# A two-layer encoder on one core: passes over zeros at the start, zero-filled keys, products in runs, new orders

## The chip, the cores and the metric

The kernel runs on one core of a Trainium2 chip. The metric is the device time of one execution in microseconds (us). Three runs of the kernel before took 853.88, 853.45 and 851.22 us; their median is 853.45 us. One more execution was taken with the hardware profiler and has its own time, 852.3 us, of which 850.5 us lie between its first and its last instruction (the span).

## The reference, cut to what matters

256 tokens of 1024 channels go through two layers and a last norm, all in float32.

```python
for i in range(2):
    h = rms_norm(x, norm_mix[i])
    x = x + (even_mixer(h, ...) if i == 0 else odd_mixer(h, ...))
    x = x + cross_attention(rms_norm(x, norm_cross[i]), mem_n, wq, wkv, wo)   # 4 heads, 256 memory tokens
    x = x + square(relu(rms_norm(x, norm_mlp[i]) @ w_up)) @ w_down            # 1024 -> 4096 -> 1024
return rms_norm(x, final_norm)

def even_mixer(h, ...):              # one projection, two groups of its columns
    hy, cq, ckv, kr = split(h @ w_in)
    z = hyena(short_conv(hy))        # two gated long convolutions, done here as products with a DFT table
    o = latent_attention(rms_norm(cq) @ w_uq, rms_norm(ckv) @ w_ukv, kr)      # 8 heads
    return concat(z, o) @ w_out

def odd_mixer(h, ...):               # 8 heads, each with two maps over 64 channels
    q, k, v = split(h @ w_qkv); q, k = rope(q), rope(k)
    p = softmax(q @ k^T / 8)         # 16 maps of 256 x 256
    a = p[:, 0] - lam * p[:, 1]      # the two maps of a head
    return (rms_norm(a @ v) * 0.8...) @ w_out
```

## The kernel before, in words

Every float32 matrix is split into a high and a low part of type fp32r (`split`: ScalarE, called ACT in the profile, rounds to the high part; VectorE, called DVE, subtracts it to get the low part). A product is three passes over TensorE (PE): high by high, high by low, low by high (`mm3`, lines 113 to 117). Each pass loads a block of 128 columns as weights (PEld in the profile) and streams up to 512 columns past it into a PSUM bank. Weights come from HBM by DMA on SyncE's queue (SP), are split, and are held in small rings of buffers (`weight`, line 91).

Where the activations are the weights' partner, their high and low parts lie side by side, so that one pass of 512 columns with the high weights (line 229) and one of 256 columns with the low weights (line 225) do the work of three (`side_by_side`). `proj_w4` makes four output banks so, in four quarters of the contraction: per bank and 128 rows of the contraction a 512-column pass H is followed by a 256-column pass L, and at the last 128 rows L stands before H. It serves the up-projections of both MLPs (8 each) and the queries of both cross-attentions (2 each); `mem_k2` does the same for the keys of the first cross-attention.

The first stage is `lat_proj` (line 496). x arrives in four pieces, the weights of the latent projection in four quarters (`lat_raw`, line 154), all on SyncE's queue. For each quarter `tr_gain` transposes two blocks of 128 channels of x on PE into one PSUM bank and takes them out with the norm's gain on ACT and DVE; the quarter of the weights is split; the products of the quarter before follow. ACT squares and sums the rows of x (line 509), GpSimd (POOL) turns the sums into 1/rms (lines 510, 511, tile `rs0`), and PE spreads `rs0` over a block (line 514) before the first chunk of the hyena projection (`hy_chunk`, H0) starts. `latents` squares the latents with `rs0` as scale (line 528).

What follows is written as lists of letters (`ORDER_EVEN`, `ORDER_CROSS`, `ORDER_ODD`); each letter calls one step. The lists set the order in which the steps are recorded; a scheduler then interleaves them, and what stands on each engine is executed in that order, each instruction waiting for its inputs.

In the odd mixer, `qkv` brings queries and keys to a form with channels on partitions: 128 partitions hold the two maps of a head, 64 each. `od_a` (A) makes the scores of one head: for each half of the tokens and each map an `mm3` over 64 rows and 256 columns, 12 passes, into one bank for each map; then the two softmaxes and the difference. B multiplies by the values, C norms, W is the output projection.

Of the kernel before, what the change touches and what calls it, by code (L numbers as in the profile page):

```python
# [17 lines left out]
P = 128  # L18
D = 1024
# [15 lines left out]
ORDER_ODD = "Q2 Q0 Q1 A0 A1 B0 A2 C0 B1 B2 Q4 C1 C2 Q3 A3 A4 Q5 A5 B3 B4 C3 A6 C4 B5 B6 C5 A7 W0 W1 C6 B7 C7"  # L35
# [3 lines left out]
def tile_encoder(ctx: ExitStack, tc: tile.TileContext, a: dict, out: bass.AP):  # L39
# [102 lines left out]

    pack = const(cst, "cpack", [P, 184])
# [22 lines left out]
    zero = T(cst, [P, 1], F32, "zero")  # L166
    nc.gpsimd.memset(zero, 0.0)
    junk = T(cst, [P, D], BF16, "junk")
# [38 lines left out]
    def proj_x(h, half, k0, nk, n, banks, first, last):  # L207
        hh, hl = h[:2]
        wh, wl = (v3(z[:, :nk * n], nk) for z in half)
        for k in range(nk):  # L210
            for t in range(2):
                sl = (slice(None), k0 + k, slice(t * P, (t + 1) * P))
                mm3(banks[t][:, :n], (hh[sl], hl[sl]), (wh[:, k, :], wl[:, k, :]),
                    first and k == 0, last and k == nk - 1)
# [8 lines left out]
    def side_by_side(b, w, both, kk):  # L223
        def low():
            nc.tensor.matmul(b[:, :256], w[1], both[:, kk, 0, :], start=False, stop=False)  # L225

        if kk == 7:
            low()
        nc.tensor.matmul(v3(b, 2), w[0], both[:, kk], start=kk == 0, stop=kk == 7)  # L229
        if kk < 7:  # L230
            low()

    def proj_w4(h, src, banks, gi, mid=None):
        both = h[2]
        for i in range(4):
            wh, wl = (v3(z, 2) for z in weight(src[i], gi=(gi, 2 * i)))
            for c in range(4):
                for k in range(2):
                    side_by_side(banks[c], [z[:, k, c * P:(c + 1) * P] for z in (wh, wl)], both, 2 * i + k)
            if mid is not None and i == 0:  # L240
                mid()
# [52 lines left out]
    def mem_k2(l, u):  # L294
        bs = [wk(), wk()]
        for i in range(2):
            wh, wl = (v3(z, 4) for z in weight(a["xa_wk"][l, u, i]))
            for c in range(2):
                for k in range(4):
                    side_by_side(bs[c], [z[:, k, c * P:(c + 1) * P] for z in (wh, wl)], memB, 4 * i + k)  # L300
# [129 lines left out]
    def softmax_e(sc, scale=None):  # L430
# [6 lines left out]
        su = col(2)  # L437
# [46 lines left out]

    def tr_gain(u):
        b = hb()
        for k in range(2 * u, 2 * u + 2):
            for t in range(2):
                o = (k % 2) * 256 + t * P
                nc.tensor.transpose(b[:, o:o + P], xt[t][:, k * P:(k + 1) * P], ident)  # L490
        for k in range(2 * u, 2 * u + 2):
            z, g = b[:, (k % 2) * 256:(k % 2 + 1) * 256], gcol[:, 0, k:k + 1]
            nc.scalar.activation(h[0][:, k, :], z, AF.Identity, bias=zero, scale=g)
# [62 lines left out]
    hs = {}  # L556
# [298 lines left out]
    qkT = {}  # L855

    def qkv(i):
# [23 lines left out]
        for u in range(2):  # L881
# [5 lines left out]
            dT = [T(op, [P, 2, 256], F32R, f"qkT{part}{i_}", bufs=3) for i_ in range(2)]  # L887
            split(*dT, b)
# [4 lines left out]
    def od_a(hd):  # L893
# [5 lines left out]
        es_, su = [], []  # L899
        bs = [wk(), wk()]  # L900
# [5 lines left out]
        for b in bs:  # L906
            e3, s_ = softmax_e(b)
            es_.append(e3)
            su.append(s_)
        w = col(2)  # L910
        nc.vector.reciprocal(w, su[1])
        nc.vector.scalar_tensor_tensor(w, w, nlam, su[0], op0=ALU.mult, op1=ALU.mult)
        eps = T(op, [P, 2], F32, "eps", bufs=4)
        nc.vector.scalar_tensor_tensor(eps, su[0], SUBLN_EPS, su[0], op0=ALU.mult, op1=ALU.mult)
        for t in range(2):
            nc.vector.scalar_tensor_tensor(a3[:, t, :], es_[1][:, t, :], w[:, t:t + 1], es_[0][:, t, :],
# [183 lines left out]
```

## Time and profile before

| | |
|---|---|
| median of three runs | 853.45 us |
| profiled execution | 852.3 us |
| its span | 850.5 us |
| PE busy | 829.4 us, 98% |
| DVE busy | 586.6 us, 69% |
| ACT busy | 508.2 us, 60% |
| POOL busy | 19.5 us, 2% |

The busy time of PE counts a pass from its start to its modelled end, and passes overlap: a 512-column pass is shown with 0.39 us while the next starts 0.23 us after it. What a pass costs in a stream is therefore the distance between two starts. The PE has its first pass at 4.60 us and works to 844.9 us; the last 5 us are the final norm and the output's DMA.

### The profile page before, as it was taken

To read this page: it belongs to the slowest core of one execution; us is meant where nothing else is said; L and a number is where in the kernel's file an instruction comes from. 1 tells how busy PE (TensorE), PEld (TensorE's weight loads), DVE (VectorE), ACT (ScalarE), POOL (GpSimd) and SP (SyncE) were. 2 spreads that over 40 slices of the span, in tenths; PEclk is the share of its full clock that TensorE was granted. 3 is DMA by queue.
4 is the path that set the end of the run, shared out by engine and by line. 5 is a ranking of instruction groups with operands and counts; after the bars stand their busy time and mean duration, and the time that the engine had idled before them with its cause. 6 is when DMAs were issued, how large, how long until landed. Compare 5 with 4: busy or idle time off the path is not lost.

```text
span 850.5 us, 12079 instructions
## 1 busy us (share of the span) xinstructions
PE 829.4 (98%) x4514; PEld 695.0 (82%) x4514; DVE 586.6 (69%) x940; ACT 508.2 (60%) x883; POOL 19.5 (2%) x51
## 2 busy tenths in 40 slices
PE   6999999999999999999999999999999999999996
PEld 5867587788888888888888788889998888888885
DVE  4978796876658666666668888677654776666663
ACT  5896464766447555555567667666543755555542
POOL 0010000000000000000000010100000000000000
PEclk9999999999999999999999999999999999999998
DMA  7660317765527666666647416245522566656641
GB/s 275 199 207 19 121 36 263 236 209 159 170 68 218 202 187 190 192 191 186 196 132 226 153 66 198 75 145 178 159 90 100 168 201 189 189 191 184 191 125 50
DMA packets 39519, 138.89 MB, mean 163 GB/s; under 512 B 4515, under 2 KB 5155, under 8 KB 39461
## 3 DMA queue, kind: packets, MB, share of 16 engines
q1 hardware_dynamic: 39460, 138.13, 51.6%
q8 instruction: 35, 0.57, 0.3%
q14 instruction: 24, 0.19, 0.1%
HBM read 137.06 MB, written 1.05 MB: 162 GB/s over the span
## 4 chain that ended last, share of the span: by engine, by line
PE 79%; issue 11%; ACT 4%; DVE 2%; DMA 2%; POOL 1%; SPq 0%; POOLq 0%; ACTq 0%; DVEq 0%
PE h L115 12%; PE h L116 12%; PE h L117 12%; PE b L229 11%; PE b L225 5%; PE h L229 4%; PE f L229 3%; PE b L115 2%; PE h L225 2%; PE b L116 2%; PE b L117 2%; PE f L115 2%; PE f L116 2%; PE f L117 2%; PE f L225 2%
## 5 line engine op out<-in xcount | busy, mean ns | idle before, releaser
L111 DVE TENSOR_TENSOR wlo<-wraw,whi 128x1024 fp32r<-128x1024 f32 (+1 forms) x127 | 153.9, 1218 | 100.9 <-ACT whi L110 100.3
L110 ACT CAST whi<-wraw 128x1024 fp32r<-128x1024 f32 (+1 forms) x127 | 132.5, 1048 | 124.0 <-PE f L229 42.7
L105 ACT ACTIVATE whi<-wraw,zero,cpack 128x512 fp32r<-128x512 f32 x208 | 160.0, 811 | 62.6 <-PE h L117 20.3
L106 DVE SCALAR_TENSOR_TENSOR wlo<-wraw,cpack,whi 128x512 fp32r<-128x512 f32 x208 | 150.3, 749 | 42.8 <-ACT whi L105 42.6
L229 PE MATMUL b<-t,whi 128*128 128x512 f32 x336 | 119.5, 398 | 0.0
L117 PE MATMUL h<-whi,ul 128*128 128x512 f32 x256 | 99.9, 390 | 0.0
L115 PE MATMUL h<-whi,uh 128*128 128x512 f32 x256 | 99.6, 389 | 0.0
L116 PE MATMUL h<-wlo,uh 128*128 128x512 f32 x256 | 99.6, 389 | 0.0
L225 PE MATMUL b<-t,wlo 128*128 128x256 f32 x336 | 87.3, 280 | 0.0
L115 PE MATMUL h<-whi,t 128*128 128x512 f32 x192 | 76.8, 401 | 0.0
L116 PE MATMUL h<-wlo,t 128*128 128x512 f32 x192 | 76.5, 399 | 0.0
L117 PE MATMUL h<-whi,t 128*128 128x512 f32 x192 | 76.0, 397 | 0.0
L229 PEld LDWEIGHTS b<-t,whi 128*128 128x128 f32 x336 | 61.1, 188 | 12.2
L229 PE MATMUL h<-t,whi 128*128 128x512 f32 x192 | 67.9, 400 | 1.4 <-DVE t L111 1.4
L225 PEld LDWEIGHTS b<-t,wlo 128*128 128x128 f32 x336 | 63.4, 189 | 3.7
L116 PEld LDWEIGHTS h<-wlo,uh 128*128 128x128 f32 x256 | 48.0, 188 | 10.1
L117 PEld LDWEIGHTS h<-whi,ul 128*128 128x128 f32 x256 | 48.1, 188 | 9.9
L115 PEld LDWEIGHTS h<-whi,uh 128*128 128x128 f32 x256 | 48.1, 188 | 9.3
L225 PE MATMUL h<-t,wlo 128*128 128x256 f32 x192 | 50.0, 281 | 0.0
L229 PE MATMUL f<-t,whi 128*128 128x512 f32 x112 | 42.7, 398 | 0.0
L117 PEld LDWEIGHTS h<-whi,t 128*128 128x128 f32 x192 | 36.1, 188 | 7.2 <-DVE t L111 0.2
L115 PEld LDWEIGHTS h<-whi,t 128*128 128x128 f32 x192 | 36.1, 188 | 7.0
(325 smaller groups left out, 1633.1 us busy)
## 6 DMA issues: line engine op xcount, KB each, us to landing
wraw<-in_mlp_up_dram SPq DMA_DIRECT2D x64, 512.0 KB, 4.2
wraw<-in_mlp_down_dram SPq DMA_DIRECT2D x64, 512.0 KB, 4.3
wraw<-in_od_w_qkv_dram SPq DMA_DIRECT2D x24, 512.0 KB, 4.3
wraw<-in_xa_wq_dram SPq DMA_DIRECT2D x16, 512.0 KB, 4.1
wraw<-in_xa_wo_dram SPq DMA_DIRECT2D x16, 512.0 KB, 4.2
wraw<-in_w_hy_dram SPq DMA_DIRECT2D x12, 512.0 KB, 4.0
wraw<-in_w_out_ev_dram SPq DMA_DIRECT2D x8, 512.0 KB, 4.4
wraw<-in_xa_wv_dram SPq DMA_DIRECT2D x8, 512.0 KB, 5.4
```

Source lines behind the costliest of these rows:

```text
L105: nc.scalar.activation(h_, r_, AF.Identity, bias=zero, scale=g)
L106: nc.vector.scalar_tensor_tensor(l_, r_, g, h_.bitcast(F32), op0=ALU.mult, op1=ALU.subtract)
L110: nc.scalar.copy(hi, src)
L111: nc.vector.tensor_tensor(lo, src, hi.bitcast(F32), op=ALU.subtract)
L115: nc.tensor.matmul(o, lh, rh, start=first, stop=False)
L116: nc.tensor.matmul(o, lh, rl, start=False, stop=False)
L117: return nc.tensor.matmul(o, ll, rh, start=False, stop=last)
L225: nc.tensor.matmul(b[:, :256], w[1], both[:, kk, 0, :], start=False, stop=False)
L229: nc.tensor.matmul(v3(b, 2), w[0], both[:, kk], start=kk == 0, stop=kk == 7)
```

## The change

Five things. (1) A tile of zeros (`junk`) is set by POOL first, and PE makes 8 passes of 512 columns over it before x is there, and 6 more after the first quarter of x. ACT runs one tiny activation at the start, so that its table is loaded then, and the four quarters of the latent weights are asked for on ACT's queue. Each block of x gets its own bank in `tr_gain`. The first hyena features are made after the third quarter's products, and the squares of x are held back until after the last gain on ACT (`tc.issue_after`). (2) `side_by_side` now makes runs: within a quarter all H passes of the four banks and then all L passes, in the next quarter L before H; in the last quarter it goes bank by bank. (3) The keys of the odd mixer are stored with zeros (`apart`): map 0 fills partitions 0 to 63 of the first 256 columns, map 1 partitions 64 to 127 of the second 256, and the rest is zero. One `mm3` of 128 rows and 512 columns then gives both maps of a head for one half of the tokens: 6 passes per head in place of 12, and the bank holds both maps of 128 tokens in place of one map of 256. (4) Writing the keys so takes two splits of 64 partitions where there was one of 128, and POOL sets six tiles of 128x1024 to zero. (5) The lists of letters change at a few places.

```diff
-ORDER_EVEN = "X J H0 L U K G R S0 D H1 F0 S1 T0 S2 S3 P0 O0 O1 O2 H2 S4 O3 H3 T1 F1 S5 S6 O4 O5 Y S7 H4 P1 H5 O6 O7 M W"
+ORDER_EVEN = "X J H0 L U K R S0 G D H1 F0 S1 T0 S2 P0 S3 O0 O1 O2 H2 S4 O3 H3 T1 F1 S6 S5 O4 O5 Y S7 H4 P1 H5 O6 O7 M W"
-    "Q0 V0 K0 K1 S0 B0 K2 S1 Q1 K3 S2 W0 V2 B1 S3 B2 B3 W1",
+    "Q0 V0 K0 K2 S0 K1 B0 V2 S1 Q1 K3 S2 B1 W0 S3 B2 B3 W1",
-ORDER_ODD = "... Q3 A3 A4 Q5 A5 B3 B4 C3 A6 C4 B5 B6 C5 A7 W0 W1 C6 B7 C7"
+ORDER_ODD = "... Q3 A3 A4 Q5 B3 A5 B4 C3 A6 C4 B6 B5 C5 A7 W0 W1 C6 B7 C7"
...
+    nc.gpsimd.memset(junk[:, :640], 0.0)
+    nc.scalar.activation(T(cst, [P, 1], F32, "first"), zero, AF.Identity, bias=zero, scale=1.0)
+    def wake(n):
+        b = hb()
+        for i in range(n):
+            nc.tensor.matmul(b, junk[:, :128], junk[:, 128:640], start=i == 0, stop=i == n - 1)
+    wake(8)
...
-            nc.sync.dma_start(lat_raw[i], a["w_lat"][i])
+            nc.scalar.dma_start(lat_raw[i], a["w_lat"][i])
...
-    def side_by_side(b, w, both, kk):
...
+        every = range(len(banks))
+        for cs in [(c,) for c in every] if last else [every]:
+            for one in (low, high) if k0 // nk % 2 else (high, low):
+                for c in cs:
+                    for k in range(nk):
+                        one(c, k)
...
+            if q == 0:
+                wake(6)
             if q:
-                proj_x(h, ws[q - 1], 2 * (q - 1), 2, 416, lat, q == 1, False)
-            if q == 2:
-                features_1()
+                z = proj_x(h, ws[q - 1], 2 * (q - 1), 2, 416, lat, q == 1, False)
+        with tc.issue_after(z.ins):
+            features_1()
         proj_x(h, ws[3], 6, 2, 416, lat, False, True)
         ssq = col(2)
-        for t in range(2):
-            nc.scalar.activation(junk, xt[t], AF.Square, accum_out=ssq[:, t:t + 1])
+        with tc.issue_after(hs["X"].ins):
+            for t in range(2):
+                nc.scalar.activation(junk, xt[t], AF.Square, accum_out=ssq[:, t:t + 1])
...
+                dT = apart[(2 * j + u) % 3]
+                for m in range(2):
+                    half = slice(64 * m, 64 * m + 64)
+                    split(*(z[half, :, m * 256:(m + 1) * 256] for z in dT), b[half])
...
-        for t in range(2):
-            for m in range(2):
-                rows = slice(64 * m, 64 * m + 64)
-                mm3(bs[m][:, t * 256:(t + 1) * 256], [z[rows, c, t * P:(t + 1) * P] for z in q], [z[rows, c, :] for z in k],
-                    True, True)
+        for t in range(2):
+            b = wk()
+            mm3(b, [z[:, c, t * P:(t + 1) * P] for z in q], [z[:, c, :] for z in k], True, True)
+            es_.append(softmax_e(b, None, su[:, t, :])[0])
```

ACT in the first stage, before: the squares (L509) stand between the gains (L493) and the splits of the latent weights, and the casts of the first hyena weights (`wraw`, 128x1024) among the last gains.

```order
L509 ACTIVATE junk_90,col_44_228<-t_2_72 128x1024
L493 ACTIVATE t_5_75<-h_129,zero_88,cpack_70 128x256
L110 CAST whi_163<-t_6_76 128x832
L493 ACTIVATE t_5_75<-h_154,zero_88,cpack_70 128x256
L110 CAST whi_200<-t_6_76 128x832
L509 ACTIVATE junk_90,col_44_228<-t_3_73 128x1024
L493 ACTIVATE t_5_75<-h_154,zero_88,cpack_70 128x256
L493 ACTIVATE t_5_75<-h_191,zero_88,cpack_70 128x256
L110 CAST whi_241<-wraw_239 128x1024
L493 ACTIVATE t_5_75<-h_191,zero_88,cpack_70 128x256
L110 CAST whi_271<-wraw_269 128x1024
```

The same place now (L506 are the gains, L525 the squares, `wraw_262` and `wraw_292` the two halves of the first hyena weights):

```order
L110 CAST whi_211<-t_10_91 128x832
L110 CAST whi_264<-wraw_262 128x1024
L110 CAST whi_294<-wraw_292 128x1024
L506 ACTIVATE t_9_90<-h_201,zero_70,cpack_85 128x256
L506 ACTIVATE t_9_90<-h_206,zero_70,cpack_85 128x256
L525 ACTIVATE junk_72,col_51_251<-t_6_87 128x1024
L110 CAST whi_382<-wraw_380 128x768
L525 ACTIVATE junk_72,col_51_251<-t_7_88 128x1024
L110 CAST whi_388<-wraw_386 128x768
L544 ACTIVATE t_63_334,col_61_332<-b_126,rs_19_110 128x256
```

Both casts of the hyena weights now stand ahead of the last two gains, and both squares behind them. On PE the pass that spreads `rs0` still stands between the last latent product and H0.

PE in an up-projection of the first MLP, before (`b` and `f` are output banks, `t` the activations):

```order
L229 MATMUL b_2827<-t_491_2395,whi_2833 128x512
L225 MATMUL b_2827<-t_491_2395,wlo_2834 128x256
L229 MATMUL b_2828<-t_491_2395,whi_2833 128x512
L225 MATMUL b_2828<-t_491_2395,wlo_2834 128x256
L229 MATMUL b_2828<-t_491_2395,whi_2833 128x512
L225 MATMUL b_2828<-t_491_2395,wlo_2834 128x256
```

and now (L239 is H, L243 is L; two rows in one are the two blocks of the quarter):

```order
L239 MATMUL b_2850<-t_498_2418,whi_2856 128x512 x2
L239 MATMUL b_2851<-t_498_2418,whi_2856 128x512 x2
L239 MATMUL b_2852<-t_498_2418,whi_2856 128x512 x2
L239 MATMUL f_2853<-t_498_2418,whi_2856 128x512 x2
L243 MATMUL b_2850<-t_498_2418,wlo_2857 128x256 x2
L243 MATMUL b_2851<-t_498_2418,wlo_2857 128x256 x2
L243 MATMUL b_2852<-t_498_2418,wlo_2857 128x256 x2
L243 MATMUL f_2853<-t_498_2418,wlo_2857 128x256 x2
```

Eight H in a row, then eight L. Over the whole program the places where an L directly follows an H fall from 611 to 107 of 704.

PE at the scores of one head in the odd mixer, before (half of a head's 12 passes, between passes of the projection):

```order
L117 MATMUL h_4890<-whi_4953,t_774_3977 128x512
L115 MATMUL b_4974<-qkT_935_4678,qkT_961_4808 128x256
L116 MATMUL b_4974<-qkT_936_4679,qkT_961_4808 128x256
L117 MATMUL b_4974<-qkT_935_4678,qkT_962_4809 128x256
L115 MATMUL b_4974<-qkT_935_4678,qkT_961_4808 128x256
L116 MATMUL b_4974<-qkT_936_4679,qkT_961_4808 128x256
L117 MATMUL b_4974<-qkT_935_4678,qkT_962_4809 128x256
L115 MATMUL h_5166<-whi_5172,t_800_4100 128x512
```

and now (half of a head's 6 passes):

```order
L905 MATMUL b_4826<-cpack_85,t_958_4805 128x128
L115 MATMUL b_4837<-apart_813_4130,qT_854_4339 128x512
L116 MATMUL b_4837<-apart_814_4131,qT_854_4339 128x512
L117 MATMUL b_4837<-apart_813_4130,qT_855_4340 128x512
L116 MATMUL h_4889<-wlo_4934,t_781_4000 128x512
```

Three passes of 512 columns over all 128 rows stand where six of 256 columns over 64 rows stood.

## Rows read from the trace of the kernel before

**Rows 1.** The page, part 1: busy us, share and instructions.
```profile
PE 829.4 (98%) x4514; PEld 695.0 (82%) x4514; DVE 586.6 (69%) x940; ACT 508.2 (60%) x883; POOL 19.5 (2%) x51
```

**Rows 2.** PE's timeline, first 24 us: start us, us, what.
```profile
4.60 2.04 PE L490 MATMUL h<-cpack,t 128*128 128x128 f32 x8 [4.60 <-DMA t<-in_x_dram]
...
13.63 0.55 PE L117 MATMUL b<-whi,t 128*128 128x416 f32 x1
...
15.79 0.35 PE L117 MATMUL b<-whi,t 128*128 128x416 f32 x1
...
23.18 0.36 PE L115 MATMUL h<-t,whi 128*128 128x256 f32 x1
```

**Rows 3.** Timeline of all engines, 6 to 24 us: ACT, POOL, SP.
```profile
7.37 0.56 ACT L493 ACTIVATE t<-h,zero,cpack 128x256 fp32r<-128x256 f32 x1
...
8.90 0.97 SPq L95 DMA_DIRECT2D wraw<-in_w_hy_dram  x2
...
15.88 1.05 ACT L509 ACTIVATE junk<-t 128x1024 bf16<-128x1024 f32 x1
...
17.40 0.71 POOL L511 TENSOR_TENSOR rs<-col,mhalf 128x2 f32<-128x2 f32 x1
...
18.95 1.04 ACT L110 CAST whi<-wraw 128x1024 fp32r<-128x1024 f32 x1
```

**Rows 4.** DMA issues at 9.5 us: the second hyena half.
```profile
wraw<-in_w_hy_dram SPq DMA_DIRECT2D x1, 512.0 KB, 7.0
```

**Rows 5.** PE's waits in the whole span: total us, times, longest.
```profile
PE b L115 <- ACT t L553: 0.9, 1, 0.9
PE b L117 <- DVE latT L111: 0.8, 1, 0.8
...
PE b L115 <- ACT t L110: 0.7, 1, 0.7
```

**Rows 6.** PE's timeline, one up-projection, 289.17 to 300.43 us.
```profile
289.17 0.39 PE L229 MATMUL b<-t,whi 128*128 128x512 f32 x1
...
297.64 0.40 PE L229 MATMUL b<-t,whi 128*128 128x512 f32 x1
...
298.58 0.39 PE L225 MATMUL b<-t,wlo 128*128 128x256 f32 x2
298.80 0.63 PE L229 MATMUL b<-t,whi 128*128 128x512 f32 x2
299.27 0.40 PE L225 MATMUL b<-t,wlo 128*128 128x256 f32 x2
...
300.43 0.39 PE L115 MATMUL h<-whi,uh 128*128 128x512 f32 x1
```

**Rows 7.** The page, part 5: weight loads of the L passes.
```profile
L225 PEld LDWEIGHTS b<-t,wlo 128*128 128x128 f32 x336 | 63.4, 189 | 3.7
```

**Rows 8.** PE's timeline at two blocks of scores, odd mixer.
```profile
476.23 0.40 PE L116 MATMUL h<-wlo,t 128*128 128x512 f32 x1
...
476.78 0.28 PE L117 MATMUL b<-qkT,qkT 64*128 64x256 f32 x1
476.79 0.28 PE L116 MATMUL b<-qkT,qkT 64*128 64x256 f32 x1
...
478.06 0.50 PE L117 MATMUL h<-whi,t 128*128 128x512 f32 x1
...
479.55 0.39 PE L117 MATMUL h<-whi,t 128*128 128x512 f32 x1
479.87 0.38 PE L115 MATMUL b<-qkT,qkT 64*128 64x256 f32 x1
...
480.78 0.50 PE L115 MATMUL h<-whi,t 128*128 128x512 f32 x1
481.12 0.39 PE L116 MATMUL h<-wlo,t 128*128 128x512 f32 x1
```

**Rows 9.** Odd mixer: PE, PEld, DVE, ACT, POOL busy, clock, DMA.
```profile
455.00:560.00 105.00, 104.34 (x575) 84.40 (x574) 83.44 (x163) 68.05 (x164) 7.55 (x16) 1.00 0.43 134
```

More of the change, by code (lines that the diff above doesn't have):

```diff
@@ L141, in const @@
         return t
+    zero = T(cst, [P, 1], F32, "zero")
+    nc.gpsimd.memset(zero, 0.0)
+    junk = T(cst, [P, D], BF16, "junk")
+    nc.gpsimd.memset(junk[:, :640], 0.0)
[5 more added lines that the diff above has]
+    wake(8)
     pack = const(cst, "cpack", [P, 184])
@@ L212, in proj_x @@
                 sl = (slice(None), k0 + k, slice(t * P, (t + 1) * P))
-                mm3(banks[t][:, :n], (hh[sl], hl[sl]), (wh[:, k, :], wl[:, k, :]),
-                    first and k == 0, last and k == nk - 1)
+                z = mm3(banks[t][:, :n], (hh[sl], hl[sl]), (wh[:, k, :], wl[:, k, :]),
+                        first and k == 0, last and k == nk - 1)
+        return z
     def proj_xs(h, src, n, banks, gi=None, mid=None, at=0):
@@ L221, in proj_xs, with side_by_side, high, low @@
                 mid()
-    def side_by_side(b, w, both, kk):
[L224 to L231, printed above, removed]
+    def side_by_side(banks, w, both, k0):
+        wh, wl = w
+        nk = wh.shape[1]
+        last = k0 + nk == 8
+        def high(c, k):
+            nc.tensor.matmul(v3(banks[c], 2), wh[:, k, c * P:(c + 1) * P], both[:, k0 + k],
+                             start=k0 + k == 0, stop=last and k == nk - 1)
+        def low(c, k):
+            nc.tensor.matmul(banks[c][:, :256], wl[:, k, c * P:(c + 1) * P], both[:, k0 + k, 0, :],
+                             start=False, stop=False)
+        every = range(len(banks))
[4 more added lines that the diff above has]
+                        one(c, k)
     def proj_w4(h, src, banks, gi, mid=None):
-        both = h[2]
         for i in range(4):
[L236 to L239, printed above, removed]
+            w = [v3(z, 2) for z in weight(src[i], gi=(gi, 2 * i))]
+            side_by_side(banks, w, h[2], 2 * i)
             if mid is not None and i == 0:
@@ L296, in mem_k2 @@
         for i in range(2):
[L297 to L300, printed above, removed]
+            side_by_side(bs, [v3(z, 4) for z in weight(a["xa_wk"][l, u, i])], memB, 4 * i)
         y = joined(*bs)
@@ L436, in softmax_e @@
         e3 = v3(t2(), 2)
-        su = col(2)
+        su = col(2) if su is None else su
         for m in range(2):
@@ L483, in tile_encoder @@
     rs0 = T(ep, [P, 2], F32, "rs0")
+    hs = {}
     def tr_gain(u):
-        b = hb()
         for k in range(2 * u, 2 * u + 2):
+            z, g = hb()[:, :256], gcol[:, 0, k:k + 1]
             for t in range(2):
[L489 to L493, printed above, removed]
+                nc.tensor.transpose(z[:, t * P:(t + 1) * P], xt[t][:, k * P:(k + 1) * P], ident)
+            hs["X"] = nc.scalar.activation(h[0][:, k, :], z, AF.Identity, bias=zero, scale=g)
             nc.vector.scalar_tensor_tensor(h[1][:, k, :], z, g, h[0][:, k, :].bitcast(F32), op0=ALU.mult, op1=ALU.subtract)
@@ L855, in tile_encoder @@
     qkT = {}
+    apart = [[T(op, [P, 2, 512], F32R, f"apart{i}{j}", bufs=1) for j in range(2)] for i in range(3)]
+    for z in apart:
+        for y in z:
+            nc.gpsimd.memset(y.bitcast(F32), 0.0)
     def qkv(i):
@@ L886, in qkv @@
                     nc.tensor.transpose(b[:, c, t * P:(t + 1) * P], rows[t][:, cs], ident)
-            dT = [T(op, [P, 2, 256], F32R, f"qkT{part}{i_}", bufs=3) for i_ in range(2)]
-            split(*dT, b)
+            if part == 0:
+                dT = [T(op, [P, 2, 256], F32R, f"qT{i_}", bufs=3) for i_ in range(2)]
+                split(*dT, b)
+            else:
+                dT = apart[(2 * j + u) % 3]
+                for m in range(2):
+                    half = slice(64 * m, 64 * m + 64)
+                    split(*(z[half, :, m * 256:(m + 1) * 256] for z in dT), b[half])
             qkT[part, 2 * j + u] = dT
@@ L898, in od_a @@
         a3 = v3(av, 2)
[L899 to L900 removed]
+        es_ = []
+        su = T(op, [P, 2, 2], F32, "su", bufs=4)
         for t in range(2):
[L902 to L909 removed]
+            b = wk()
+            mm3(b, [z[:, c, t * P:(t + 1) * P] for z in q], [z[:, c, :] for z in k], True, True)
+            es_.append(softmax_e(b, None, su[:, t, :])[0])
         w = col(2)
[L911 to L912 removed]
+        nc.vector.reciprocal(w, su[:, :, 1])
+        nc.vector.scalar_tensor_tensor(w, w, nlam, su[:, :, 0], op0=ALU.mult, op1=ALU.mult)
         eps = T(op, [P, 2], F32, "eps", bufs=4)
[L914 removed]
+        nc.vector.scalar_tensor_tensor(eps, su[:, :, 0], SUBLN_EPS, su[:, :, 0], op0=ALU.mult, op1=ALU.mult)
         for t in range(2):
[L916 removed]
+            nc.vector.scalar_tensor_tensor(a3[:, t, :], es_[t][:, 1, :], w[:, t:t + 1], es_[t][:, 0, :],
                                            op0=ALU.mult, op1=ALU.add)
```

8 lines of the change are left out of this document (2 added, 6 removed).

## The prediction

> **What bounds the kernel now.** I read the page's busy shares first: PE is busy for 829.4 of 850.5 us [rows 1], so the time is PE's work, pass after pass, plus the places where PE stands. Then I read PE's timeline, taking the distance between two starts as the price of a pass, and PE's waits. They are few: in the whole span no wait behind the first stage is over 1.1 us in one piece, and the larger of those that the change touches are 0.9, 0.8 and 0.7 us [rows 5]. The other large one (1.4 us in all, on DVE at the head of the first cross-attention's query projection) lies behind the same chain of ACT instructions in both programs, and I leave it. So a gain comes in three ways: fewer or cheaper passes, an earlier start of the hyena chunk H0 (now 23.18 us [rows 2]), or a wait that goes. ACT and DVE matter where PE waits for them: that is so in the first 35 us and hardly later.
>
> **The start.** Before, PE waits for x until 4.60 us, and its passes of 416 columns are slow up to about 15 us: 0.55 us each, against 0.35 later [rows 2]. That is the engine at the lower of its two clock levels; it rose only after PE had gone over to products that follow each other nearly without a break. The 8+6 passes over zeros lie in time in which PE has nothing, so they cost nothing, and the products may run at the upper level from their first. Worth up to 2 us if PE set the end of this stage. In the changed program it doesn't. The pass that spreads `rs0` stands in PE's queue ahead of H0, `rs0` needs both squares of x, and these now stand on ACT behind the last two gains, which stand behind the casts of both hyena weight halves. So H0 waits for this chain:
> - The second hyena half was issued at about 9.5 us (the second of two from 8.90) and landed 7.0 us later, at 16.5 us [rows 3, 4]. The transfers ahead of it are the same bytes as before; ACT's queue only takes four of them over. I take 16.3 us.
> - Its cast: 1.04 us [rows 3], of which 0.1 overlaps the next: 17.3.
> - Two gains of 0.56 us, overlapping by 0.1 [rows 3]: 18.2.
> - Square 1.05, a cast of 768 columns, about 0.75 of 1.04 [rows 3], square 1.05 and the read of its sum, 0.2: 21.3.
> - POOL's two steps, about 1.0 until 0.71 us after 17.40 [rows 3]: 22.3; the spreading pass: H0 at about 22.7.
> That is 0.5 us earlier than 23.18. If both halves land 2 us earlier, H0 is at 20.7 (PE is then the next limit: 48 products of 416 columns at 0.19 us, 416/512 of 0.23, and 16 transposes behind x); if ACT's queue, which must wait for the first latent quarter before it may ask for the third, holds everything up, it may come 1 us late. From -2.5 to +1; I take -0.5.
>
> Behind H0 PE stood 0.8 us for the low part of `latT` and 0.9 us for the copy that frees a bank [rows 5]. PE's new order has eight more products of the next hyena chunk between the two uses of `latT`, 8 x 0.12 = 1 us of cover, and ACT comes to these copies at about the same time as before, since it has two casts more in front and fewer behind. I take 1.3 us off, between 0 and 1.7. The rest of the even mixer keeps its chains; the order on DVE hardly differs around the spectra. 0, with 1 us to either side.
>
> **The cross-attention of layer 0.** One wait of 0.7 us is for ACT's split of probabilities that sits behind the values' splits [rows 5]: V2 came just before B1. Now V2 stands ahead of S1. With the restart this is 0.9 us; between 0 and 1.5.
>
> **The runs.** One up-projection before: 24 alternating pairs from 289.17 to 297.64 us, 8.47/24 = 0.353 us a pair, then the last eight, which alternate only half of the time, from 297.64 to 300.43, 0.349 a pair [rows 6]. In these an L before an L takes 0.11 (two in 0.22 us) and an H before an H 0.235 (two in 0.47): 0.345 for a pair of like neighbours. So a pair that moves into runs saves 0.004 to 0.008 us; over the neighbours of the whole trace it is 5.5 ns. 611-107 = 504 pairs move (the last quarter stays as it was): 504 x 5.5 ns = 2.8 us. From below: if long runs bring nothing, 0; from above 504 x 0.012 = 6 us, if H came down to the 0.227 us of the 512-column passes of the down-projections. DVE and ACT are no part of this: in the MLPs PE never waits for them.
>
> **The scores.** A block of six 64-row passes, half a head: PE would go on at 479.78 (a 512-column pass from 479.55 takes 0.23), the first pass of full height starts at 480.78, and takes 0.34 in place of 0.23 [rows 8]: 1.0+0.11 = 1.11 us. The blocks of the trace are seven of six passes at 1.11, one of 17 and one of 18, where passes of the two maps start in pairs (476.78 and 476.79), at 478.06-476.46+0.11 = 1.7 and 1.8 [rows 8], one of eight at 1.0, two of four at 0.8, and three single ones at 0.5: 7.8+3.5+1.0+1.6+1.5 = 15.4 us for 96 passes. Now there are 48 passes of 512 columns, of full height as their neighbours, at 0.227: 10.9 us. That saves 4.5 us. Bounds: 6 if the three-pass groups let the copies around them start earlier too, 0 if a change of weights between unlike streams costs as much as the change of height did.
>
> *Here a rule of the Trainium skill speaks against the change.* "TensorE: Matmul & The Clock Gate", Part 3 on packing small matmuls, says that passes on disjoint groups of rows of the array run at the same time, and that a pass over few rows takes as long as a full one, so that packing is the gain. The paired starts above agree with it. By that rule alone the 96 passes are 48 pairs of 256 columns, 48 x 0.12 = 5.7 us, and one wide product per pair, 10.9 us, would lose 5.2 us. But only two of the 15 blocks pair up; in the others a pass waits for its own group, and every change of height costs 0.1 us going in and 0.1 coming out. By the blocks the sum is -4.5, by the rule +5.2.
>
> What the zeros cost: four key blocks are split by 64 partitions, so 4 more ACT copies and 4 more DVE subtractions of 512 elements, about 0.6 and 0.7 us each, 2.4 and 2.8 us in all. DVE has 83.4 and ACT 68.1 busy of 105 us in this stage [rows 9], and PE has products of the projections and of the next layer's memory to do meanwhile. POOL's six memsets of 1024 elements: not in the trace; they stand around the step that makes the odd mixer's 1/rms, needed only when the first projection is done, and POOL is busy for 7.6 of 105 us there [rows 9]. I charge 0.3 us for the tighter stage; between 0 and 2.
>
> **The sum.** -0.5 -1.3 -0.9 -2.8 -4.5 +0.3 = -9.7 us on the profiled execution's 852.3 us (span 850.5 and 1.8 around it): 842.6 us. The median of the runs is 1.15 us above that execution, so I predict 843.7 us for the median after. Bounds of the parts, taken as partly independent, give 839 to 848.
>
> **Rivals.**
> 1. *The start gives more.* The first weights asked for at once bring the hyena halves earlier too, and PE at the upper clock level from the first product sets the pace: H0 at 20.7, 2 us more, 841.7. For it: the DMA engines work from about 2 us on, and the casts are early enough then. Against: the same bytes through the same engines.
> 2. *The scores give nothing or lose*, by the concurrency above: the stage keeps its 15.4 us or pays 5.2, and the time is 848 to 853.4, at the end no measurable change. For it: the paired starts. Against: 15.4 us as they stand, counted with all entries.
> 3. *The change doesn't do what it says outside the scores.* Zeros, runs and orders bring nothing (the clock wasn't on the path, like neighbours were no better, waits reappear one step later), -4.2 in all: 849.3. For it: the difference of neighbours is 5 ns of 353.
> 4. *Slower: the runs of L become bound by their weight loads.* The load of an L's weights is shown with 189 ns [rows 7]; before, it had an H of 0.23 us in front of it nearly always. In a run each L of 0.11 us has only the L before it as cover. If the load is exposed, an L costs 0.189: about 500 like neighbours x 0.075 = +38 us, and the time is 853.45-6.9+38 = 884. It decides from 19 ns per L on, where it takes back the 9.7. Against: the pairs of L that stand in the last quarter already start 0.11 us apart.
>
> **How the numbers follow.** Forecast as summed 62%, rival 1 10%, rival 2 10%, rival 3 14%, rival 4 4%. No change is what a measurement of this kernel can't tell, within 0.3% or 2.6 us. The forecast and rival 1 are faster; rival 3 is faster at 849.3 but may end inside the bound; rival 2 about half. So faster 0.89, same 0.07, slower 0.04. The range of 838.5 to 849.5 us holds the first, second and most of the third case.
>
> **What would show it.** After: H0's first 256-column pass at 22 to 23 us, with the spreading pass directly before it waiting for POOL, and products of 416 columns at the upper clock level from the first. Like neighbours of H at 0.227 to 0.235 and of L at 0.115 in the MLPs, so that an up-projection takes 11.1 in place of 11.26 us. 48 score passes of 512 columns 0.23 apart, and an odd mixer about 4.5 us shorter. The wait for the split probabilities in the first cross-attention gone. I am wrong if H0 starts after 23.5, if an L in a run costs 0.12 or more, if the odd mixer's PE waits for DVE or ACT more than 1 us longer than before, or if a wait that isn't in the profile now appears in the even mixer or the first cross-attention because a step was moved.

## The result, and the profile after

Predicted 843.7 us; measured 843.28 us, the median of four runs (842.26 to 844.68), against 853.66 of the kernel before (851.22 to 854.27, four runs). The ratio is 0.9885, 95% interval [0.9864, 0.9906]: 8.0 to 11.6 us faster. The profiled execution after has a span of 842.1 us, 8.4 less than the one before. The total came out within 0.5 us, but not because each term did: the odd mixer gave 3 us less than forecast, and the stretch from H0 to the first MLP gave over 2 us more.

The busy line of the page after, to be read against [rows 1]:

```profile
PE 825.1 (98%) x4480; PEld 692.5 (82%) x4480; DVE 593.4 (70%) x944; ACT 513.1 (61%) x888; POOL 25.1 (3%) x58
```

PE is still the bound. DVE and ACT have 6.8 and 4.9 us more to do. The new keys and their copies make 2.3 and 2.6 us of it (b1_keys_alone, below, against before), and without the products in runs it is 3.6 and 2.1 us less (e2_no_runs). PE's timeline of the start answers to [rows 2]; columns are start us, us, then what runs and in brackets what it waited for:

```profile
1.43 3.60 PE L152 MATMUL h<-junk 128*128 128x512 bf16 x8 [1.43 <-POOL junk L146]
6.17 0.30 PE L505 MATMUL h<-cpack,t 128*128 128x128 f32 x1 [1.14 <-DMA t<-in_x_dram]
...
10.64 0.35 PE L117 MATMUL b<-whi,t 128*128 128x416 f32 x1
...
20.93 0.71 PE L530 MATMUL h<-cpack,rs 128*128 128x128 f32 x4 [0.40 <-POOL rs L527]
21.40 0.36 PE L115 MATMUL h<-t,whi 128*128 128x256 f32 x1
```

The products of 416 columns take 0.35 us from the first that follows another, where before they took 0.55 until 15 us. The spreading pass waits for POOL, as forecast, and H0 is at 21.40, ahead of the forecast 22.7. It is not the usual value: of five more executions with the same program up to the first MLP, below, four have 22.3 to 22.6, and p1_pairs has 23.75, which is later than before.

The up-projection that answers to [rows 6]:

```profile
284.06 1.52 PE L239 MATMUL b<-t,whi 128*128 128x512 f32 x6
285.42 0.62 PE L239 MATMUL f<-t,whi 128*128 128x512 f32 x2
285.87 0.88 PE L243 MATMUL b<-t,wlo 128*128 128x256 f32 x6
286.59 0.40 PE L243 MATMUL f<-t,wlo 128*128 128x256 f32 x2
...
295.19 0.39 PE L115 MATMUL h<-whi,uh 128*128 128x512 f32 x1
```

Six H in 1.36 us are 0.227 each, six L in 0.72 are 0.120, and the whole takes 11.13 in place of 11.26 us. Three score passes, which answer to [rows 8]:

```profile
475.09 0.39 PE L117 MATMUL h<-whi,t 128*128 128x512 f32 x1
475.32 0.39 PE L115 MATMUL b<-apart,qT 128*128 128x512 f32 x1
475.55 0.40 PE L116 MATMUL b<-apart,qT 128*128 128x512 f32 x1
475.79 0.40 PE L117 MATMUL b<-apart,qT 128*128 128x512 f32 x1
476.02 0.39 PE L115 MATMUL h<-whi,t 128*128 128x512 f32 x1
```

They run 0.23 us apart, and here the neighbours of full height pay nothing. PE's waits between 23 and 260 us, first of an execution before (us in total, times, longest):

```profile
PE h L229 <- DVE t L111: 1.1, 1, 1.1
PE b L115 <- ACT t L553: 0.9, 1, 0.9
PE b L117 <- DVE latT L111: 0.8, 1, 0.8
PE f L116 <- DVE wlo L111: 0.8, 1, 0.8
PE b L115 <- ACT t L110: 0.7, 1, 0.7
```

and then of the changed kernel, in its second profile (r_changed):

```profile
PE h L190 <- DVE t L295: 1.0, 1, 1.0
PE h L481 <- DVE hy L595: 0.5, 1, 0.5
...
```

In this execution all five larger waits of before are gone, those that the prediction named and two that it left alone; the wait at L190 (transposes of x at the end of the even mixer) is 0.5 longer. The first profile of the same program, whose H0 was a microsecond earlier, still has the wait at the queries (L239), and one behind ACT at `latT`:

```profile
PE h L239 <- DVE t L111: 1.3, 2, 0.8
PE b L115 <- ACT latT L110: 0.9, 1, 0.9
```

By stages, from the starts of the same passes in each trace. "Before" also has b1_keys_alone, which is the kernel before up to the odd mixer; "changed" also r_changed, e3, e4, e5 and p1, which are the changed kernel up to there.

| stretch | before | changed | forecast | measured |
|---|---|---|---|---|
| start to H0 | 23.18, 22.23 | 21.40, 22.34, 22.64, 22.32, 22.37, 23.75 | -0.5 | -0.2 of the means |
| H0 to the first up-projection | 232.2, 232.8 | 229.1, 227.3, 226.4, 227.1, 227.8, 227.5 | -2.7 | -5.0 |
| both MLPs | 356.2 | 354.0 | -2.0 | -2.2 |
| odd mixer and second cross-attention | 230.8 | 229.5, 229.2 | -4.4 | -1.5 |

(The forecast's 2.8 us for the runs is shared out by their passes: 512 of 704 pairs are in the MLPs.) Behind the second MLP's last product there are 8.2 us in both; PE's last product of before ends at 842.7 us, not at 844.9 as said in the section on time and profile before.

### The profile page after: what moved, and what is told of

It reads as the page before. It is cut to its first block, busy times and chain, and to the rows that moved or that the text cites. A ratio compares the mean times of both kernels' runs of the same rounds, so it can differ in the third digit from the quotient of the medians.

```text
span 842.1 us, 12032 instructions
## 1 busy us (share of the span) xinstructions
PE 825.1 (98%) x4480; PEld 692.5 (82%) x4480; DVE 593.4 (70%) x944; ACT 513.1 (61%) x888; POOL 25.1 (3%) x58
## 4 chain that ended last, share of the span: by engine, by line
PE 76%; issue 11%; ACT 6%; DMA 3%; DVE 2%; POOL 1%; SPq 0%; POOLq 0%; ACTq 0%
PE h L115 11%; PE h L117 11%; PE h L116 11%; PE b L239 11%; PE b L243 6%; PE h L239 4%; PE f L239 3%; PE b L115 2%; PE h L243 2%; PE b L117 2%; PE b L116 2%; PE f L115 2%; PE f L117 2%; PE f L116 2%; PE f L243 2%
## 5 line engine op out<-in xcount | busy, mean ns | idle before, releaser
L116 PE MATMUL h<-wlo,uh 128*128 128x512 f32 x256 | 99.6, 389 | 0.0
L239 PE MATMUL b<-t,whi 128*128 128x512 f32 x336 | 90.7, 392 | 0.0
L116 PE MATMUL h<-wlo,t 128*128 128x512 f32 x192 | 76.2, 397 | 0.0
L239 PEld LDWEIGHTS b<-t,whi 128*128 128x128 f32 x336 | 59.3, 189 | 9.0
L116 PEld LDWEIGHTS h<-wlo,uh 128*128 128x128 f32 x256 | 48.1, 188 | 10.1
L243 PEld LDWEIGHTS b<-t,wlo 128*128 128x128 f32 x336 | 49.8, 190 | 4.7
L243 PE MATMUL b<-t,wlo 128*128 128x256 f32 x336 | 53.5, 282 | 0.0
L239 PE MATMUL h<-t,whi 128*128 128x512 f32 x192 | 51.2, 395 | 1.5 <-DVE t L111 1.5
L116 PEld LDWEIGHTS h<-wlo,t 128*128 128x128 f32 x192 | 36.2, 188 | 6.5
L239 PEld LDWEIGHTS h<-t,whi 128*128 128x128 f32 x192 | 33.5, 188 | 7.8 <-DVE t L111 2.8
```

Source lines behind the costliest of these rows:

```text
L116: nc.tensor.matmul(o, lh, rl, start=False, stop=False)
L239: nc.tensor.matmul(v3(banks[c], 2), wh[:, k, c * P:(c + 1) * P], both[:, k0 + k], start=k0 + k == 0, stop=last and k == nk - 1)
L243: nc.tensor.matmul(banks[c][:, :256], wl[:, k, c * P:(c + 1) * P], both[:, k0 + k, 0, :], start=False, stop=False)
```

## The experiments

Kernels of one job share the runs of the kernel before; its medians were 852.37, 852.84 and 852.85 us in the three jobs. Ratios are to those.

**e1_no_zeros.** The passes over zeros are left out.

```diff
-    wake(8)
...
-            if q == 0:
-                wake(6)
```

> The changed kernel without its 8+6 passes over zeros; all else as changed. In the changed kernel the hyena chunk starts at 21.40 us, PE's last latent product begins at 20.18 and the spreading pass at 20.93, behind POOL's rs0. Theory A (PE at the upper clock level is half of the gain of the start): without the zeros the products of 416 columns are 0.35 us apart until about 15 us, some 12 to 15 of them by 0.16 us more, and PE ends its products 2 to 2.4 us later, at 22.5; H0 starts at 23.0 to 23.5 and the time is 1.6 to 2.1 us over the changed kernel's, about 845. Theory B (the prediction's: ACT's chain to rs0 sets H0 and the zeros lie beside it): H0 at 21.4 to 21.9 and no more than 0.5 us lost.

Measured: 844.80 us, ratio 0.9910 [0.9895, 0.9924]; H0 at 22.57, between the two theories, and no later than the 22.3 to 22.6 of most executions with zeros. PE's last slow product stands at 12.82, the next are at the upper level:

```profile
12.82 0.55 PE L117 MATMUL b<-whi,t 128*128 128x416 f32 x1
13.17 0.40 PE L115 MATMUL b<-whi,t 128*128 128x416 f32 x1
13.41 0.35 PE L116 MATMUL b<-wlo,t 128*128 128x416 f32 x1
...
22.57 0.36 PE L115 MATMUL h<-t,whi 128*128 128x256 f32 x1
```

The first up-projection starts at 250.94, behind other waits (0.8 at L668, 0.8 at L189); with zeros it starts between 249.04 and 251.25, on average of six at 250.0. The two ratios with and without zeros overlap. So the zeros are worth between nothing and about 2 us, and the runs don't settle how much.

**r_changed and p2_more_zeros.** The changed kernel again, and with 13 passes ahead of x.

```diff
-    wake(8)
+    wake(13)
```

> The changed kernel again, beside the others of this job. In its first profile TensorE was at the upper clock level from 5.68 us on without a break and H0 started at 21.40; in three kernels with the same first stage the level rose at 4.85, fell at 8.26, rose again at 11.7, and H0 started at 22.3 to 22.6. Theory A (the 8 passes end before x is there, PE has nothing for 1.1 to 1.75 us, and whether the level holds hangs on how late x lands): this run shows one of the two, H0 at 21.4 with the level held or 22.3 to 22.7 with the level lost. Theory B (the first profile was the rule): level held and H0 at 21.4 again. The time: 842.5 to 844.5 us.

> The changed kernel with 13 in place of 8 passes over zeros ahead of x, so that PE has work until x is there. Theory A (the gap before x lets the level fall in some executions): the level holds from about 5 us on, H0 at 21.2 to 21.8, and the median 0.3 to 1.0 us under the changed kernel's of this job. Theory B (ACT's chain behind the second hyena half sets H0, and the level is worth nothing beyond it): H0 as in the changed kernel within 0.3 us, and the zeros, if they last longer than x takes to land, cost up to 0.8 us.

Measured: 843.01 (ratio 0.9885 [0.9868, 0.9902]) and 842.79 us (0.9886 [0.9871, 0.9901]). In r_changed H0 is at 22.34, and the second group of passes over zeros takes 2.25 us for six, where the first profile has 1.3:

```profile
7.99 2.42 PE L152 MATMUL h<-junk 128*128 128x512 bf16 x6
10.24 1.09 PE L505 MATMUL h<-cpack,t 128*128 128x128 f32 x8
```

So theory A holds, though the view shows a granted clock of 1.00 here: by their distance, 0.38 us against 0.21, these passes are at the lower level. In e3_old_keys, whose x landed 0.6 us later, the view shows the fall itself, between 8.5 and 12 us (length, busy us by engine, granted clock, DMA share, GB/s), and in its timeline six passes over zeros then take 2.3 us and stand ahead of the transposes, for which ACT waits in turn:

```profile
8.50:12.00 3.50, 3.50 (x14) 2.35 (x13) 2.40 (x4) 2.36 (x6) 0.00 (x0) 0.55 1.06 399
```

```profile
6.76 0.30 PE L505 MATMUL h<-cpack,t 128*128 128x128 f32 x1 [1.75 <-DMA t<-in_x_dram]
7.61 0.55 PE L505 MATMUL h<-cpack,t 128*128 128x128 f32 x3 [0.55 <-DMA t<-in_x_dram]
8.00 2.50 PE L152 MATMUL h<-junk 128*128 128x512 bf16 x6
10.29 1.72 PE L505 MATMUL h<-cpack,t 128*128 128x128 f32 x8
...
10.97 1.02 ACT L506 ACTIVATE t<-h,zero,cpack 128x256 fp32r<-128x256 f32 x2 [1.14 <-PE h L505]
```

0.55 is close to the lower level, half of full speed. With 13 passes the same stretch is at 1.00 and H0 at 21.53:

```profile
8.50:12.00 3.50, 3.33 (x20) 2.69 (x19) 3.21 (x6) 3.50 (x8) 0.00 (x0) 1.00 1.05 400
```

So theory A of p2 holds for the level and for H0, but the time doesn't follow. With H0 at 21.53 the wait at L190 is 1.4 us, at 22.34 it is 1.0, at 22.64 (e3) 0.2, and the first up-projection starts at 249.67, 249.61 and 249.04. This is no rule: the first profile has its H0 at 21.40, only 0.3 at L190 and its up-projection at 250.48, and e5 has 22.37, 0.2 and 250.17. All that the executions show is that an earlier H0 need not arrive at the first MLP; where it goes differs, and why stays open.

**e2_no_runs.** H and L alternate again.

```diff
+        for c in range(len(banks)):
+            for k in range(nk):
+                for one in (low, high) if k0 + k == 7 else (high, low):
+                    one(c, k)
```

> The changed kernel with H and L alternating as before (an H and an L per block and bank). Theory A: each of the two MLPs is 1.1 us longer again (178.8 in place of 177.7 us), an up-projection takes 11.26 us, the second layer's stages too, in all 2.5 to 3 us over the changed kernel, about 846. Rival: the shorter MLPs come from elsewhere, and the time stays within 0.5 us of the changed kernel's 843.3.

Measured: 844.94 us, 0.9910 [0.9896, 0.9925], and the MLPs 178.79 and 177.36 us, to 0.01 us those of before, against 177.70 and 176.27. Theory A in the MLPs, where the runs are worth 2.2 us. Outside them nothing is seen: from H0 to the first up-projection e2 takes 227.40 us and in the odd mixer's stretch 229.03, no more than the kernels with runs, and the whole is 1.7 to 1.9 us over the changed kernel's two medians, not 2.5 to 3.

**b1_keys_alone.** The kernel before with the keys, score passes and softmaxes of the change.

```diff
-            split(*dT, b)
...
+                dT = apart[(2 * j + u) % 3]
+                for m in range(2):
+                    half = slice(64 * m, 64 * m + 64)
+                    split(*(z[half, :, m * 256:(m + 1) * 256] for z in dT), b[half])
```

> The kernel before with the zero-filled keys, 48 score passes and softmaxes of the change and nothing else of it. Theory A (the passes save 3.3 us and the waits that come with the keys give 2 of them back): the stage from the end of the first MLP to the second layer's first up-projection takes 229.3 to 230 us (before: 230.8), and the whole is 1 to 1.5 us faster than before. Theory B (in the order of before the keys bring their full price, as the prediction had it): 226.5 us, 4.2 faster. Rival by concurrency of the two halves: 5 us slower.

Measured: 851.21 us (11 runs), 0.9980 [0.9971, 0.9990], 1.6 us; the stage 229.08 against 230.82. Theory A, the stage a little under its range. The score passes with what they do to their neighbours cost 11.8 us against 15.4, 3.6 less; PE's other lost time in the stage (starts further apart than the usual of their kind) is 7.1 us against 5.1. Its waits there, of which before showed only one of 0.5 in its busiest 105 us:

```profile
PE b L953 <- DVE t L951: 1.0, 3, 0.5
PE h L115 <- ACT t L954: 0.4, 1, 0.4
PE b L939 <- ACT t L941: 0.4, 2, 0.2
```

These lines are the norm of a head's output and its way back to PE. They come to 1.8 us, against 0.8 in the whole stage before; by the distances between starts, the places with a wait hold 1.4 of the 2.0 us. In windows of 105 us DVE is busy 86.2 us in place of 83.4 and ACT 72.6 in place of 68.1 [rows 9].

**e3_old_keys.** The changed kernel with the 96 passes of before.

```diff
-            mm3(b, [z[:, c, t * P:(t + 1) * P] for z in q], [z[:, c, :] for z in k], True, True)
+            for m in range(2):
+                rows = slice(64 * m, 64 * m + 64)
+                mm3(bs[m][:, t * 256:(t + 1) * 256], ...)
```

> The changed kernel with the keys, scores and softmaxes of before (96 passes over 64 rows), but with the new order of steps. Between the end of the first MLP and the first up-projection of the second, the changed kernel takes 229.5 us (before: 230.8); its 48 score passes cost 12.1 us with their edges (before, 15.4), but other places of the stage stand 2.1 us longer. Theory A (those 2.1 us come with the zero-filled keys: more copies on ACT and DVE, a bank that holds both maps): the stage is 230.5 to 231 us and the whole 1 to 1.5 us slower than the changed kernel. Theory B (they come with the new order of letters): the stage is 232.5 to 233, the whole 3 to 3.5 us slower.

Measured: 844.29 us, 0.9904 [0.9887, 0.9921]; the stage 230.74, as theory A has it. The blocks cost 15.5 us again and the other lost time is 5.1, as before: the 2 us of waits come with the keys.

**e4_maps_in_turn** and **p1_pairs.** The rule that passes on disjoint rows run at the same time, tried: the two maps of a head in turn, then held to that order.

```diff
+            for i, (il, ir) in enumerate(((0, 0), (0, 1), (1, 0))):
+                for m in range(2):
+                    with tc.issue_after(prev.ins):
+                        prev = nc.tensor.matmul(bs[m][:, t * 256:(t + 1) * 256], ...)
```

> As e3_old_keys, but the passes of the two maps of a head are issued in turn (upper 64 rows, lower 64 rows, upper, ...), three of each for one half of the tokens. Theory A (what the two long blocks of before hinted: neighbours on disjoint halves of the array start together, and only passes of the same half wait for each other): six passes cost 3 x 0.12 to 0.15 and 0.2 for the two changes of height, 0.56 to 0.65 us against 1.11 before and 0.70 with the zeros; the 96 passes cost 9 to 10.5 us, and the kernel is 2 to 4 us faster than e3_old_keys and 0 to 3 faster than the changed kernel. Theory B (a 64-row pass costs 0.15 whatever stands beside it): the same as e3_old_keys within 0.5 us.

> The changed kernel with keys and softmaxes of before, and the 12 passes of a head held to the order lower map, upper map, lower, ... by issue_after, behind two passes of 64 columns that only wait for the two banks and are written over. In e4_maps_in_turn the order on PE took most heads apart again into six passes of one map; where the maps did alternate, two passes started 0.003 us apart and the next two 0.118 later. Theory A (passes over disjoint halves of the rows run at the same time): a head costs 0.1 + 0.22 + 5 x 0.118 + 0.2 = 1.1 us and the two small passes 0.06 to 0.2, 9.5 to 10.5 us for 8 heads against 12.1 with the zeros, and the 2.1 us of other waits in the stage that came with the zero-filled keys go: the stage from the end of the first MLP to the second layer's first up-projection takes 225.5 to 227.5 us (changed: 229.5), the whole 2 to 4 us less than the changed kernel. Theory B (zeros are the better use): the stage at 229.5 or more.

Measured: e4 844.72 us, 0.9908 [0.9893, 0.9923]. The stage takes 231.37 us, 0.6 more than in e3: the score passes cost 14.5 us with their edges, 1.0 less, and the other lost time is 1.7 more. The scheduler took several heads apart into six passes of one map, perhaps because the banks come free one after the other: 24 of 48 possible pairs start together, where in before it was 16. Two blocks of its trace, first one that alternates for 12 passes, then one of a single map:

```profile
469.59 1.58 PE L122 MATMUL b<-qkT,qkT 64*128 64x256 f32 x17
471.10 0.50 PE L117 MATMUL h<-whi,t 128*128 128x512 f32 x1
...
472.91 0.98 PE L122 MATMUL b<-qkT,qkT 64*128 64x256 f32 x6
473.82 0.50 PE L115 MATMUL h<-whi,t 128*128 128x512 f32 x1
```

Within the first, the passes of six pairs start about 0.003 us apart, a pair every 0.117 after the first; the others follow each other at 0.12. In p1 a whole head is one block, between two small passes that wait for its banks:

```profile
508.46 0.19 PE L918 MATMUL b<-qkT,qkT 128*128 128x64 f32 x1
508.58 0.98 PE L924 MATMUL b<-qkT,qkT 64*128 64x256 f32 x12
509.49 0.30 PE L916 MATMUL b<-qkT,qkT 128*128 128x64 f32 x1
509.62 0.47 PE L115 MATMUL h<-whi,t 128*128 128x512 f32 x1
```

Twelve passes in 0.91 us, 1.16 with the small ones, against 6 x 0.232 = 1.39 with the zeros. The rule holds, and such a head is cheaper by its passes. But some heads are cut in two by other passes, so that over all eight the gain is small: 11.5 us with the edges, against 11.8 to 12.1 with the zeros. And p1 took 844.93 us (0.9913 [0.9897, 0.9929]) and its stage 231.33: other lost time is 9.4 us. Its waits in the stage:

```profile
PE b L968 <- DVE t L966: 1.4, 2, 0.7
PE b L947 <- ACT kTm L110: 1.1, 1, 1.1
```

That both softmaxes of a head can only start when all 12 passes are done may be why; this was not tried. p1's profile also has the latest start of the six: PE begins on x at 7.02 us, after a wait of 1.99, and H0 is at 23.75. Its first up-projection is at 251.25, 1.5 us after the 249.7 of the other five on average, so part of its time has nothing to do with the scores.

**e5_old_odd_order** and **e6_old_early_orders.** The changed kernel with the letters of before in the odd mixer, and in the even mixer and the cross-attentions.

```diff
-ORDER_ODD = "... Q5 B3 A5 B4 C3 A6 C4 B6 B5 C5 A7 W0 W1 C6 B7 C7"
+ORDER_ODD = "... Q5 A5 B3 B4 C3 A6 C4 B5 B6 C5 A7 W0 W1 C6 B7 C7"
```

> The changed kernel with the order of letters of before in the odd mixer, and the new keys. Measured so far for the stage from the end of the first MLP to the second layer's first up-projection: before 230.8, keys alone on before 229.1 (without runs, which are worth 0.3 to 0.4 in this stage), the changed kernel 229.2 and 229.5. Theory A (the waits of 2 us that ate part of the saving come with the keys, and the new order is worth nothing or costs 0.3): the stage at 228.7 to 229.2, the whole within 0.7 us of the changed kernel's 843.0. Theory B (the new order is what makes the keys fit): the stage at 230 or more, the whole 1 us slower or more.

> The changed kernel with the orders of letters of before in the even mixer and in both cross-attentions. From H0 to the first up-projection the changed kernel takes 227.3 to 229.1 us (five runs of the same program up to there), before 232.2 and 232.8. Theory A (the orders take away the waits behind latT, 2.0 us, the 0.9 of the output projection at 124 us, the 1.3 of the query projection at 154 us and the 0.9 of the values at 229 us): 231.5 to 232.5, and the whole 3.5 to 5 us slower than the changed kernel, about 847. Theory B (only what the prediction gave them, latT 1.3 and the values 0.9; the rest went with the banks and the earlier start): 229.5 to 230.5, the whole 2 us slower. Rival: the start alone did it, no change.

Measured: e5 843.05 us, 0.9881 [0.9867, 0.9895], the stage 228.61: theory A, the new odd order is worth nothing. It may even cost: p4, below, with the same order of before, has 228.64, and six executions with the new order (first profile, r_changed, p2, e1, e6, e8) have 229.2 to 229.6. Without runs the two orders are level (b1 229.08, e2 229.03). e6 847.22 us, 0.9929 [0.9916, 0.9942], and 230.56 from H0 to the first up-projection, 3.0 over the mean of the six. It is just over B by the stage, and A by the whole, to which the late H0 adds. Its waits show which of the five come back:

```profile
PE h L239 <- DVE t L111: 1.4, 3, 0.8
...
PE f L116 <- DVE wlo L111: 0.8, 1, 0.8
PE b L115 <- ACT t L110: 0.7, 1, 0.7
```

Those at the output projection, the values and the queries; not the two behind `latT`, although the letters of before are back there. e6's H0 is late, at 23.37, so whether the new first stage or the late start keeps these two away is not shown. The wait at the queries isn't safely gone: the first profile of the changed kernel has 1.3 us of it and e5 0.9; r_changed, e3, e4 and p1 have none.

**e8_weights_on_sp.** The latent weights on SP's queue again.

```diff
-            nc.scalar.dma_start(lat_raw[i], a["w_lat"][i])
+            nc.sync.dma_start(lat_raw[i], a["w_lat"][i])
```

> The changed kernel with the four quarters of the latent weights asked for on SP's queue, between the pieces of x, as before. In the changed kernel the second hyena half is asked for at 8.04 to 8.63 us and lands at 14.7 to 15.3, where the prediction took 16.3. Theory A (ACT's queue lets SP ask for the hyena halves 1 to 1.3 us sooner, and ACT's chain behind them sets H0): the half lands at 16.0 to 16.6, H0 1.0 to 1.5 us later, 23.2 to 23.8; the whole 0.3 to 1.3 us slower, since later waits take up a part. Theory B (the bytes ahead of it decide, not the queue): it lands within 0.3 us of 15, H0 unchanged.

Measured: 843.93 us, 0.9891 [0.9879, 0.9904]. The half was asked for at 9.55 and landed 7.2 us later, at 16.7, about as theory A says. But H0 stands at 20.78, earlier than in any other, because the scheduler now put ACT's squares ahead of the casts of the hyena halves:

```profile
15.91 1.05 ACT L525 ACTIVATE junk<-t 128x1024 bf16<-128x1024 f32 x1
...
17.08 1.06 ACT L525 ACTIVATE junk<-t 128x1024 bf16<-128x1024 f32 x1
...
18.14 1.98 ACT L110 CAST whi<-wraw 128x1024 fp32r<-128x1024 f32 x2
```

So this isn't a trial of the queue alone. It shows one price of ACT's queue all the same: PE has the first quarter of x at 4.82 us, as it had at 4.60 and 3.98 in before and b1, where the kernels with the weights on ACT's queue start on it at 6.2 to 7.0:

```profile
4.82 1.06 PE L505 MATMUL h<-cpack,t 128*128 128x128 f32 x4
```

Here PE comes to x straight from the passes over zeros, and its last latent product, at 20.23, not ACT's chain, sets H0. The early H0 is lost again at `latT` (waits of 0.8 and 0.6 us behind ACT), and the first up-projection starts at 250.08.

**p4_odd_order_zeros.** e5 with 13 passes over zeros.

> The changed kernel with the odd mixer's order of before and 13 passes over zeros ahead of x: what the runs so far point to as the best of the parts. If both are worth what the stages say (0 to 0.7 us from the order, 0 to 0.3 from the level that holds), 842.0 to 843.0, at most 1 us under the changed kernel; if the new order is needed, 844.

Measured: 842.56 us (842.31 to 842.90), 0.9878 [0.9866, 0.9891]. Half a microsecond under e5 in the same job, with overlapping intervals: no version was shown to beat the changed kernel.

## Why the prediction was right, and where it was not

- **The start, -0.5: the size is not shown.** The means differ by 0.2 us, and each side spreads by over 1 us; p1's 23.75 lies behind the 23.5 that the text gave as a sign of being wrong. ACT's chain was the right one, with errors in two links. The second hyena half landed at 14.7 to 15.3 us, not 16.3, since SP asked for it at 8.0 to 8.6 and not 9.5. And "the same bytes" left out that the latent weights on ACT's queue now come beside x: x is there at 6.17 to 7.02 in place of 4.60, so PE stands between the passes over zeros and x. Where the level is then low, the second group of zeros, forecast to cost nothing, takes 1.8 to 2.6 us (1.3 in the first profile) ahead of the transposes that ACT's gains wait for. The products of 416 columns did run at the upper level nearly from the first, as forecast, but they began 1.5 to 2.9 us later than in the first profile.
- **The waits behind H0, -1.3: right in kind, small in size.** Both went in r_changed, and the distances between starts say 2.0 us before. In the first profile, with H0 at 21.40, 0.9 us at `latT` is left.
- **The rest of the even mixer, 0: failed.** The wait of PE at the first stage of the output projection (L116, 0.8 us in [rows 5]'s view) was taken for untouched; the letters removed it, as e6 shows. So was the one at the queries (1.1 to 1.4 us), which went in four of six executions. In the table this is most of the 2.3 us beyond the forecast of that stretch.
- **The values of layer 0, -0.9: right.** The wait of 0.7 went with the letters.
- **The runs, -2.8: right in the MLPs,** 2.2 us against 2.0; the 0.8 us for the other pairs is not shown by any run. And it came by other parts: an H in a run is 0.227, 0.008 less, and an L 0.120, 0.003 more. The text had said that an L of 0.12 would prove it wrong; that bound, which was met, was set without the gain of H beside it. Rival 4, L bound by its weight load of 0.189, is out.
- **The scores, -4.5: mis-sized.** The blocks of before cost the 15.4 us that were counted, but the new passes are 0.232 apart and not 0.227, and with their neighbours cost 11.8 to 12.1: -3.3 to -3.6.
- **The tighter stage, +0.3: the step that failed most.** It measured +2.0 (7.1 to 7.4 us of other lost time against 5.1, in b1 and in the changed kernel alike, and 5.1 again in e3). The text said that PE has other products to do meanwhile; on average it has, but at the heads' norms it waits. The bound of 2 given there just held. The new odd order, which the sum has no term for, may be 0.6 us or more of the stage.
- **Rival 2, the concurrency of the two halves: true as a mechanism and without effect here.** Before, two of fifteen blocks used it as the text says, and two more that it missed: the one of eight passes and one of those of four, 16 pairs in all. Made to use it, p1 pays 0.3 to 0.6 us less for the passes and 2 us more in waits.

Two misses of opposite sign, 2.9 us less in the odd mixer and 2.3 us more ahead of the first MLP, left the sum near, and that is luck. The range would have held either of them alone.

## What to carry to other kernels

Price a cheaper stage with its waits: when PE is shortened by some microseconds and two other engines get two to four us more each, look for the chain that is nearly late now, and charge the lost time, not the share of busy time. Where an order of steps changes, list every wait in that stretch and decide for each; a wait that is left out as untouched is a term of zero that was never worked out. Read a stage's gain at its far end, and in all executions that there are, since an early start need not arrive there. Passes that fill an idle engine are free only if they end before the work behind them is due.

## What the hardware showed that was not expected

- The clock level can be lost again within the start: after the eight passes over zeros PE waited 1.75 us for x in e3, and the granted clock was 0.55 between 8.5 and 12 us. With 13 passes it stayed at 1.00 in p2, where the second six take 1.30 us.
- The view's granted clock is not enough for the first microseconds. In before it is 1.00 from 8.5 to 15 us, where products of 416 columns start 0.35 us apart; from 15.4 us on they start 0.19 apart. There the distance between starts tells the level.
- The same program's first stage ended between 21.40 and 23.75 us in six executions, with x landing up to 0.9 us apart.
- Asking for the latent weights on a second queue let the hyena weights be asked for about 1 us sooner and made x 1.3 us or more later.
- Two passes over disjoint halves of the rows started about 0.003 us apart, and the next pair 0.117 later, for 256 columns; passes over the same half follow at 0.12.
